# Feed-forward down product of 20 of 32 tiles by seven block products for eight, with the rows of the sum streamed through SBUF

## The chip, the core and the metric

The kernel runs on one core of one Trainium2 chip. The metric is the device time of one execution in microseconds (us). TensorE multiplies into PSUM (eight banks per partition), VectorE and ScalarE take the results out of PSUM, GpSimd does a little elementwise work, and the SP queue issues the DMAs. Each engine works through its own queue in order and waits on semaphores.

## What is computed

One decoder layer for a prompt of 1024 tokens and 8 single-token samples, so 1032 columns in all, with a model width of 1024 and a feed-forward width of 4096. The part that is changed is the feed-forward block near the end:

```python
x = layer_norm(ALPHA * x + (1 + g1) * m, ln1_g, ln1_b)
v = x * (1 + sc2) + sh2
hid = jnp.square(jax.nn.relu(jnp.einsum('bld,df->blf', v, w_up)))
x = layer_norm(ALPHA * x + (1 + g2) * jnp.einsum('blf,fd->bld', hid, w_down), ln2_g, ln2_b)
```

Here `hid` is 4096 wide (32 tiles of 128 features), and the down product adds its 1024 outputs (8 rows of 128 features, `x1[0]` to `x1[7]`, each 128x1032) to the residual.

## The kernel before

All matrices are held transposed: 128 features on the partitions, 1032 columns along the row. Every fp32 operand is split into a high and a low part (`split`: ScalarE writes the high part, VectorE subtracts), and a product of a 128x128 weight tile with a tile of data is three matmuls: high by high, low by high, high by low (`term`, L210 in the profile).

`product` runs over three column blocks of 344 (`BLOCKS`). For each block it takes one PSUM tile from `psm()`, accumulates all its terms there, and calls an evacuation: ScalarE's relu for an up product (24 matmuls a block), VectorE's `gate_add` (L789, and L792 for the 8 sample columns) for a down product. `psm()` draws from a pool of four PSUM tiles of one bank each (tag `mm`); three more (`pss()`, tag `sm`) serve small products.

Weights come by DMA in a list, `order`, two ahead of their use; `parts` splits each into `whi` and `wlo` (two buffers each). The feed-forward runs in 5 groups of four up products and four `wda` weights (each for two output rows, 4 feature tiles), then 2 groups of six up products and eight `wdb` weights. All eight rows `x1` stay in SBUF. A scheduler sets the order of the queues, outside a few stretches that are written out by hand (the last one among them).

Names: L210 is the matmul of `term` (L255 after the change), L202 is `split` (L247 after), L944 the evacuation of an up product (L1047 after), L789 `gate_add` (L834 after), L1115 the matmul and L1090 the addition of the new block products.

Of the kernel before, what the change touches and what calls it, by code (L numbers as in the profile page):

```python
# [10 lines left out]
F32 = mybir.dt.float32  # L11
# [40 lines left out]
SLOTS = {"raw": 2, "whi": 2, "wlo": 2, "G": 2, "xg": 2, "yc": 2}  # L52


NFB = 2
NFA = (DFF // P - 6 * NFB) // 4

# [7 lines left out]
def cols(ap, b):  # L65
    return ap[:, b[0]:b[1]]


def build(tc, ctx, a):
# [7 lines left out]

    cp = ctx.enter_context(tc.tile_pool(name="cp", bufs=1))
    sp = ctx.enter_context(tc.tile_pool(name="sp", bufs=1))
    pm = ctx.enter_context(tc.tile_pool(name="pm", bufs=MMB, space=PSUM))  # L80
    pq = ctx.enter_context(tc.tile_pool(name="pq", bufs=7 - MMB, space=PSUM))
    dp = ctx.enter_context(tc.tile_pool(name="dp", bufs=1, space=DRAM))

# [9 lines left out]
    def tmp(w=T, dt=F32):  # L93
        return sp.tile([P, w], dt, tag="t", name=nm("t"), bufs=5)

    def psm():
        return pm.tile([P, 512], F32, tag="mm", name=nm("mm"))

    def psa():
        return pq.tile([P, 512], F32, tag="ada", name=nm("ada"), bufs=1)  # L100
# [40 lines left out]
    def part(tag, dt, w):  # L141
        return sp.tile([P, w], dt, tag=tag, name=nm(tag), bufs=SLOTS.get(tag, 1))
# [24 lines left out]
    for f in range(NFA):  # L167
        order += [("wup", i) + ((("raw", "aw", "yt"),) if i == 2 else ()) for i in range(4 * f, 4 * f + 4)]
        order += [("wda", f, mp) for mp in range(4)]
    spare = [f"U{i}" for i in range(8, 14)] + ["C0", "C1", "C2", "C3", "G", "G"]  # L170
    for f in range(NFB):
        order += [("wup", 4 * NFA + 6 * f + i) for i in range(6)]
        for m in range(8):
            tags = ("raw", spare[2 * m - 4], spare[2 * m - 3])
            order.append(("wdb", f, m) + ((tags,) if f == NFB - 1 and m > 1 else ()))
    ahead = []

    queue = []
# [9 lines left out]
    def prefetch():  # L188
        if order:
            key, raw = load_next()  # L190
            ahead.append((key, parts(*raw)))

    def weights(*key):
        if not ahead:
            prefetch()
        got, w = ahead.pop(0)
        assert got == key, (got, key)
        prefetch()
        return w
# [782 lines left out]
    for k in range(8):  # L982
        after(rescale(k, b), vcopy)

    for f in range(NFA):
        kh = [t[2] for t in two] if f == 0 else []
        kh += [hidden(4 * f + i) for i in range(len(kh), 4)]
# [6 lines left out]
    def row_shift():  # L994

        near, base = tmp(dt=F32R), tmp()
        nc.scalar.copy(near, x1[0])
        for b in BLOCKS:
            ln1.total(base, (cols(near, b),), P, b, w=rones)
        return base  # L1000

    for f in range(NFB):
        if f == NFB - 1:
            base = row_shift()
        kh = []
        for i in range(6):
            kh.append(hidden(4 * NFA + 6 * f + i))
            if f == NFB - 1:
                for m in ((0, 1), (2, 3, 4), (5, 6, 7), (), (), ())[i]:
                    tc.keep_in_program_order(tt(x1[m], x1[m], base, op=ALU.subtract))  # L1010
        kf = [(i, h, l) for i, (h, l) in enumerate(kh)]
        if f < NFB - 1:
            for m in range(8):
                product(weights("wdb", f, m), kf, lambda b, ps: gate_add(x1[m], ps, M_G2, m, b))
            continue
# [12 lines left out]
        def add_q(m, b):  # L1028
            tt(cols(qsum, b), cols(qsum, b), sq[m], op=ALU.add)

        def moments(b, xs=(), qs=()):

            mu, s, q = cols(mean, b), cols(rsum, b), cols(qsum, b)
            total(mean, (s, *(cols(x1[m], b) for m in xs)), D, b)
            act(s, mu, AF.Square)
            total(qsum, (q, *(sq[m] for m in qs)), D, b, eps)

        def variance(b):
            s, q, w = cols(rsum, b), cols(qsum, b), cols(tmp(), b)
# [24 lines left out]

        wd = []

        def down(m, b):
            product(wd[m], kf, lambda b, ps: gate_add(x1[m], ps, M_G2, m, b), (b,))
            square(m, b)

        b = LAST[0]
        for m in range(8):
            wd.append(weights("wdb", f, m))
# [133 lines left out]
```

## Time and profile before

| | |
|---|---|
| three runs | 1573.47, 1574.13 (median), 1575.65 us |
| profiled execution | 1574.45 us, its span 1572.6 us |
| TensorE busy | 1541.8 us, 98% of the span |
| VectorE busy | 868.6 us, 55% |
| ScalarE busy | 526.3 us, 33% |
| moved by DMA | 141.44 MB, mean 90 GB/s |

The span is the profiled stretch from first to last instruction. A matmul's record lasts longer than the pitch at which matmuls follow each other, since they overlap, so the pitch is read from start to start.

### The profile page before, as it was taken

Reading aid. Unit: us, or ns where it says so; the run is one execution under the profiler, and the core shown is the slowest. Engines: PE = TensorE matmul, PEld = TensorE weight load, DVE = VectorE, ACT = ScalarE, POOL = GpSimd, SP = SyncE. Lnnn points to the kernel's source line nnn. Section 1 sums busy time; section 2 is a strip of 40 time slices with the busy share of each in tenths; the row PEclk is TensorE's granted clock in tenths of the full one; section 3 lists DMA queues with packets and bytes.
Section 4 is the critical chain, followed back from the end, with each engine's and each line's share of the span. In section 5 each row is a group of like instructions: output and inputs, shape, how many; then the busy total and the mean of one; then the engine's idle time right before and its main releaser. Section 6 shows DMA issues by size and latency. Waiting matters only on the chain.

```text
span 1572.6 us, 23959 instructions
## 1 busy us (share of the span) xinstructions
PE 1541.8 (98%) x10058; PEld 1489.2 (95%) x10058; DVE 868.6 (55%) x1653; ACT 526.3 (33%) x805; POOL 169.0 (11%) x168
## 2 busy tenths in 40 slices
PE   6999999999999999999999999999999999999996
PEld 5899999999889999999999999999999999999995
DVE  4575556677876742636996444434343433335477
ACT  2553323323333353613577121121312213113334
POOL 0004222221211311100241000000000000000001
PEclk9999999999999999999999999999999999999998
DMA  9332344344343323412221111111111111111102
GB/s 366 114 118 94 108 132 141 118 140 132 135 151 128 119 96 108 175 42 93 82 68 54 41 54 41 48 47 42 53 41 54 41 54 34 45 56 51 61 31 88
DMA packets 49628, 141.44 MB, mean 90 GB/s; under 512 B 5736, under 2 KB 14696, under 8 KB 49520
## 3 DMA queue, kind: packets, MB, share of 16 engines
q1 hardware_dynamic: 49520, 139.91, 27.4%
q8 instruction: 79, 1.29, 0.3%
q14 instruction: 29, 0.24, 0.1%
HBM read 126.33 MB, written 13.56 MB: 89 GB/s over the span
## 4 chain that ended last, share of the span: by engine, by line
PE 94%; DVE 3%; DMA 1%; ACT 1%; issue 1%; POOL 0%; SPq 0%; ACTq 0%; DVEq 0%; POOLq 0%
PE mm L210 86%; PE ada L229 2%; PE sm L651 1%; PE sm L643 1%; PE sm L842 1%; PE sm L638 1%; PE sm L673 1%; PE sm L210 1%; DMA S<-in_xT 0%; PE sm L617 0%; DVE U L1055 0%; PE sm L236 0%; DMA s<-in_ssm 0%; PE sm L597 0%; PE mm L425 0%
## 5 line engine op out<-in xcount | busy, mean ns | idle before, releaser
L210 PE MATMUL mm<-U,whi 128*128 128x344 f32 x3058 | 778.5, 323 | 4.6 <-ACT U L336 4.6
L210 PEld LDWEIGHTS mm<-U,whi 128*128 128x128 f32 x3058 | 536.6, 188 | 21.4 <-issue 11.8
L210 PE MATMUL mm<-U,wlo 128*128 128x344 f32 x1529 | 488.1, 322 | 0.0
L202 ACT CAST whi<-raw 128x1024 fp32r<-128x1024 f32 (+1 forms) x122 | 125.7, 1030 | 544.0 <-PE mm L210 529.8
L210 PEld LDWEIGHTS mm<-U,wlo 128*128 128x128 f32 x1529 | 286.9, 188 | 3.0 <-issue 2.8
L789 DVE SCALAR_TENSOR_TENSOR U<-mm,mod,U 128x344 f32<-128x344 f32 (+3 forms) x216 | 122.7, 571 | 206.5 <-PE mm L210 206.5
L210 PE MATMUL mm<-S,whi 128*128 128x344 f32 (+3 forms) x912 | 232.8, 320 | 0.0
L202 DVE TENSOR_TENSOR wlo<-raw,whi 128x1024 fp32r<-128x1024 f32 (+1 forms) x122 | 146.5, 1201 | 132.2 <-ACT whi L202 131.8
L210 PEld LDWEIGHTS mm<-S,whi 128*128 128x128 f32 x912 | 160.6, 188 | 0.3
L210 PE MATMUL mm<-S,wlo 128*128 128x344 f32 (+3 forms) x456 | 145.3, 320 | 0.0
L210 PE MATMUL mm<-C,whi 128*128 128x344 f32 x516 | 143.0, 320 | 0.0
L944 DVE TENSOR_TENSOR t<-t 128x344 f32<-128x344 f32 x96 | 49.3, 515 | 87.5 <-ACT t L944 87.5
L210 PEld LDWEIGHTS mm<-C,whi 128*128 128x128 f32 x516 | 92.9, 188 | 0.1
L210 PEld LDWEIGHTS mm<-S,wlo 128*128 128x128 f32 x456 | 85.6, 188 | 0.1
L1057 POOL TENSOR_SCALAR U<-U,vec 128x392 f32<-128x392 f32 (+1 forms) x4 | 5.6, 1388 | 720.0 <-DVE U L1055 720.0
L210 PE MATMUL mm<-C,wlo 128*128 128x344 f32 x258 | 82.5, 320 | 0.0
L210 PE MATMUL mm<-G,whi 128*128 128x344 f32 x258 | 82.1, 321 | 0.1
L210 PE MATMUL mm<-xg,whi 128*128 128x344 f32 x258 | 82.0, 320 | 0.0
L387 DVE SCALAR_TENSOR_TENSOR t<-t,vec,t 128x1064 f32<-128x1064 f32 (+1 forms) x52 | 71.8, 1388 | 10.7 <-ACT t L385 9.7
L944 ACT ACTIVATE t<-mm 128x344 f32<-128x344 f32 x96 | 43.6, 455 | 97.0 <-PE mm L210 97.0
L210 PE MATMUL mm<-yc,whi 128*128 128x344 f32 x210 | 66.8, 322 | 0.0
L945 DVE TENSOR_TENSOR S<-t,S 128x344 fp32r<-128x344 f32 x66 | 33.9, 516 | 29.6 <-ACT S L944 29.3
(360 smaller groups left out, 2117.7 us busy)
## 6 DMA issues: line engine op xcount, KB each, us to landing
raw<-in_win SPq DMA_DIRECT2D x44, 512.0 KB, 3.7
aw<-in_wada SPq DMA_DIRECT2D x33, 512.0 KB, 4.2
raw<-in_wup SPq DMA_DIRECT2D x32, 512.0 KB, 3.5
raw<-in_wout SPq DMA_DIRECT2D x24, 512.0 KB, 3.5
raw<-in_wda SPq DMA_DIRECT2D x20, 512.0 KB, 3.5
G<-acd SPq DMA_DIRECT2D x16, 512.0 KB, 3.9
raw<-in_wdb SPq DMA_DIRECT2D x16, 384.0 KB, 3.1
S<-in_xT SPq DMA_DIRECT2D x8, 516.0 KB, 10.2
```

Source lines behind the costliest of these rows:

```text
L202: return nc.scalar.copy(thi, src), tt(tlo, src, thi, op=ALU.subtract)
L210: mm(ps[:, :b[1] - b[0]], wt, cols(xt, b), start=(i == 0 and q == 0), stop=(i == n - 1 and q == 2))
L229: mm(ps[32 * g:32 * g + 32, :256], cs[:, 2 * kp + k2, :], w[:, c:c + 256], start=(kp == 0), stop=(kp == KD // 2 - 1), tile_position=(0, 32 ...
L387: stt(r, t[:, k:k + n], wt(k), r, op0=ALU.mult, op1=ALU.add)
L638: mm(po[:, i * P:(i + 1) * P], st[:, h0:h0 + P], bc[2 + g][:, sl], start=True, stop=True)
L643: mm(py[r * HD:(r + 1) * HD, i * P:(i + 1) * P], xg[g][:, 0, h * HD:(h + 1) * HD], Gs[g][:, h, :], start=True, stop=True, tile_position=(0 ...
L651: mm(pst, bt[:, g * P:(g + 1) * P], xg[g][:, 1], start=True, stop=True)
L673: mm(pn[:, :BW], w, cols(src, b), start=(i == 0), stop=(i == len(srcs) - 1))
L789: stt(dst[:, lo:hi], ps[:, :hi - lo], mod[:, row + m, 0:1], dst[:, lo:hi], op0=ALU.mult, op1=ALU.add)
L842: mm(pn, w, src, start=(i == 0), stop=(i == len(srcs) - 1))
L944: return [lambda: act(x, ps, AF.Relu), lambda: tt(x, x, x, op=ALU.mult), lambda: nc.scalar.copy(xh, x), lambda: tt(xl, x, xh, op=ALU.subtr ...
L945: lambda: tt(xl, x, xh, op=ALU.subtract)]
```

## The change

Twenty of the 32 feature tiles (five groups of four) are taken by the seven-product scheme for 2x2 blocks: for a pair of output rows, four feature tiles and half the columns of the prompt, blocks of weights and of data are added and subtracted first, then seven block products replace eight. A block product is 12 matmuls of 258 columns (`QW`), 84 for a pair of rows where there were 72 of 344. Products are accumulated on top of each other in PSUM, and VectorE adds the running sum to a row after each (`add_rows`). The eight rows are stored to DRAM (`x1d`) and come back two at a time. Operands of a group are prepared by `operands`, the blocks of weights by `seven_parts`. One up product stands after each of the first two pairs of a group, one or two ahead of the group. The other twelve tiles keep the old product, six at the beginning and six at the end. `psm()` now hands out quarters of one PSUM tile of four banks, `large`, instead of four tiles, for every product of the kernel; the pairs `u` and `v` are halves of it.

```diff
-    pm = ctx.enter_context(tc.tile_pool(name="pm", bufs=MMB, space=PSUM))
+    pm = ctx.enter_context(tc.tile_pool(name="pm", bufs=1, space=PSUM))
...
+    large = pm.tile([P, MMB, 512], F32, tag="mm", name="mm")
+    turn = [0]
+
     def psm():
-        return pm.tile([P, 512], F32, tag="mm", name=nm("mm"))
+        turn[0] += 1
+        return large[:, (turn[0] - 1) % MMB]
...
-            ahead.append((key, parts(*raw)))
+            ahead.append((key, parts(*raw) if key[0] != "wds" else seven_parts(raw[0])))
...
+    def seven_parts(raw):
...
+        ha, la = part("whi", F32R, 768), part("wlo", F32R, 768)
+        hb, lb = part("U2", F32R, 1024), part("U3", F32R, 1024)
+        a11, a12, a22, a21 = (raw[:, 256 * i:256 * i + 256] for i in range(4))
+        (s1, s2), (s3, s4) = ([t[:, :256], t[:, 256:]] for t in (part("wb", F32, 512), part("wc", F32, 512)))
+        tt(s3, a11, a21, op=ALU.subtract)
...
+        pieces(raw[:, :256], ha, la, "a11")
+        pieces(s3, hb[:, :256], lb[:, :256], "s3")
...
-        for mp in range(4):
-            w = weights("wda", f, mp)
-            for m in (2 * mp, 2 * mp + 1):
-                product(w, [(4 * (m % 2) + i, h, l) for i, (h, l) in enumerate(kh)],
-                        lambda b, ps: gate_add(x1[m], ps, M_G2, m, b))
...
+        product(weights("wdb", 0, m), kf, lambda b, ps: gate_add(x1[m], ps, M_G2, m, b))
+        nc.gpsimd.tensor_copy(eight[:, m], x1[m][:, TP:])
+        dma(x1d[m], x1[m])
...
+    def hidden_raw(i):
+        r = tmp()
+        product(weights("wup", i), kv, lambda b, ps: act(cols(r, b), ps, AF.Relu))
+        tt(r, r, r, op=ALU.mult)
+        return r
...
+            split(a_[:, 0], *(x[:, c:c + QW] for x in sops["b11"]))
+            t = tmp()
+            t1, t3, t2, t4 = (t[:, i * QW:(i + 1) * QW] for i in range(4))
+            tt(t1, a_[:, 1], a_[:, 0], op=ALU.subtract)
+            tt(t3, b_[:, 1], a_[:, 1], op=ALU.subtract)
+            tt(t2, b_[:, 1], t1, op=ALU.subtract)
+            tt(t4, b_[:, 0], t2, op=ALU.subtract)
+            w = slice(2 * QW * p, 2 * QW * p + 2 * QW)
+            split(rb[:, w], *(x[:, w] for x in hl["b2"]))
+            split(t[:, :2 * QW], *(x[:, w] for x in hl["odd"]))
+            split(t[:, 2 * QW:], *(x[:, w] for x in hl["even"]))
...
+    def add_rows(ps, row, m, h):
...
+        d, g = four(row)[:, :, h], mod[:, M_G2 + m, 0:1]
+        if isinstance(ps, list):
+            for p in range(2):
+                stt(d[:, p], ps[p][:, :QW], g, d[:, p], op0=ALU.mult, op1=ALU.add)
+            return
+        if h:
+            tt(acc8[:, m], acc8[:, m], ps[:, 1, QW - NS:QW], op=ALU.add)
+        stt(d, ps[:, :, :QW], g, d, op0=ALU.mult, op1=ALU.add)
+
+    def load_rows(mp):
+        rows = [slab(f"U{4 + m % 4}") for m in (2 * mp, 2 * mp + 1)]
+        for i, r in enumerate(rows):
+            dma(r, x1d[2 * mp + i])
+        return rows
...
+            rows[0] = load_rows((mp + 1) % 4)
...
+        def multiply(ps, a_, b_, first=False):
+            for p in range(2):
+                for j in range(2):
+                    wh, wl = (t[:, j * P:(j + 1) * P] for t in w[a_])
...
+                    for q, (wt, xt) in enumerate(((wh, xh), (wl, xh), (wh, xl))):
+                        mm(pp[:, :QW], wt, xt, start=first and j == 0 and q == 0, stop=(j == 1 and q == 2),
+                           skip_group_check=not first)
...
+        u, v = (large[:, 2 * i:2 * i + 2] for i in ((1, 0) if mp % 2 else (0, 1)))
+        y = [pss(), pss()]
+        multiply(u, "a11", "b11", True)
+        add_rows(u, r1, m1, 0)
+        multiply(v, "s3", "t3", True)
+        add_rows(v, r2, m2, 1)
+        multiply(u, "s2", "t2")
+        add_rows(u, r2, m2, 0)
+        multiply(y, "a12", "b21", True)
+        add_rows(y, r1, m1, 0)
+        multiply(u, "s1", "t1")
+        add_rows(u, r2, m2, 1)
+        multiply(v, "a22", "t4")
+        add_rows(v, r2, m2, 0)
+        multiply(u, "s4", "b22")
+        add_rows(u, r1, m1, 1)
...
+            for m, r in ((m1, r1), (m2, r2)):
+                dma(x1d[m], r)
...
+        operands(0, r[0], r[1])
...
+        more = [hidden_raw(nxt[0])]
+        operands(1, r[2], r[3])
         for mp in range(4):
...
+            seven(f, mp)
+            if mp < 2:
+                turn[0] = 2 - 2 * mp
+                more.append(hidden_raw(nxt[1 + mp]))
```

The first place is TensorE's queue in an up product of the feed-forward (its three blocks begin with the data tile `yc`; `mm_...` is the PSUM tile; a bracket names the semaphore that the instruction waits for). Before:

```order
L210 MATMUL mm_10362<-yc_6815,whi_10163 128x344 [waits DVE_49,Activation_49]
...
L210 MATMUL mm_10391<-yc_6815,whi_10163 128x344 [waits Activation_49]
...
L210 MATMUL mm_10420<-yc_6815,whi_10163 128x344 [waits Activation_49]
...
L210 MATMUL mm_10458<-yc_6815,whi_10262 128x344 [waits Activation_49]
L210 MATMUL mm_10458<-yc_6815,wlo_10263 128x344 [waits DVE_49]
...
L210 MATMUL mm_10487<-yc_6815,whi_10262 128x344 [waits Activation_49]
```

The same place of the change:

```order
L255 MATMUL mm<-yc_6659,whi_8976 128x344 [waits Activation_49]
L255 MATMUL mm<-yc_6659,wlo_8977 128x344 [waits DVE_49]
...
L255 MATMUL mm<-U_685_6688,whi_8976 128x344
L255 MATMUL mm<-yc_6659,whi_8976 128x344 [waits Activation_49]
...
L255 MATMUL mm<-U_685_6688,whi_8976 128x344
L1115 MATMUL sm_9417<-S_897_9242,whi_9142 128x258 [waits Activation_49]
L1115 MATMUL sm_9418<-S_897_9242,whi_9142 128x258
L255 MATMUL mm<-yc_6659,whi_9059 128x344 [waits Activation_49]
```

A block begins with a wait for ScalarE in both. The count of the semaphore tells which evacuation is meant: before, `mm_10487` waits for the relu that reads `mm_10362`, four tiles earlier; in the change each block waits for the relu of the block just ahead of it. Two matmuls of a block product into another PSUM tile (`sm`) have moved between two blocks.

The second place is TensorE's queue in the seven block products of one pair of rows, from the second product on (12 matmuls each, the first of each shown, but for the product of `s1`, whose row reads like the first; `mm` is `large`). There is nothing like it before the change.

```order
L1115 MATMUL mm<-S_899_9244,U_891_9144 128x258 [waits DVE_49]
...
L1115 MATMUL mm<-S_901_9246,U_891_9144 128x258 [waits DVE_49]
...
L1115 MATMUL mm<-S_901_9246,whi_9142 128x258 [waits DVE_49]
...
L1115 MATMUL mm<-S_897_9242,U_891_9144 128x258 [waits DVE_49]
...
L1115 MATMUL sm_9627<-S_897_9242,whi_9391 128x258 [waits Activation_49]
L1115 MATMUL sm_9628<-S_897_9242,whi_9391 128x258
```

By their counts, each of the five products into `mm` waits for VectorE's addition (L1090) of the product just ahead, into whichever half of `large` that went. The product into `sm` of the next pair has moved behind the last one.

The third place is ScalarE's queue around the third block of an up product. Before:

```order
L944 ACTIVATE t_11891<-mm_11927 128x344 [waits PE_49]
L944 CAST S_1395_11889<-t_11891 128x344 [waits DVE_49]
L202 CAST whi_11894<-raw_11892 128x1024 [waits DMAHW2_49,PE_49,Activation_49]
L944 ACTIVATE t_11891<-mm_11956 128x344
L944 CAST S_1395_11889<-t_11891 128x344 [waits DVE_49]
```

And in the change, with `whi` the weight that is split two products ahead of its use:

```order
L1047 ACTIVATE t_11992<-mm 128x344 [waits PE_49]
L247 CAST U_1147_12079<-t_12096 128x516 [waits DVE_49]
L247 CAST whi_11995<-raw_11993 128x1024 [waits DMAHW4_49,PE_49]
L1047 ACTIVATE t_11992<-mm 128x344
L247 CAST whi_12109<-raw_12107 128x256 [waits DMAHW0_49,PE_49]
```

In both, the cast of a weight stands ahead of the evacuation of the third block, and the evacuation carries no wait of its own, because the cast waits for the same last matmul.

## Rows read from the trace of the kernel before

**Rows 1.** The page, busy time by engine: us, share of span, instructions.
```profile
PE 1541.8 (98%) x10058; PEld 1489.2 (95%) x10058; DVE 868.6 (55%) x1653; ACT 526.3 (33%) x805; POOL 169.0 (11%) x168
```
**Rows 2.** The page, the chain that ended last, shares by engine.
```profile
PE 94%; DVE 3%; DMA 1%; ACT 1%; issue 1%; POOL 0%; SPq 0%; ACTq 0%; DVEq 0%; POOLq 0%
```
**Rows 3.** Busy time by stretch: PE, PEld, DVE, ACT, POOL (instructions); clock, DMA share, GB/s.
```profile
700.00:800.00 100.00, 99.44 (x621) 97.89 (x621) 76.73 (x147) 47.64 (x76) 18.63 (x14) 1.00 0.26 80
900.00:1000.00 100.00, 100.00 (x637) 100.00 (x636) 41.28 (x80) 20.30 (x33) 0.00 (x0) 1.00 0.15 48
```
**Rows 4.** Waits of PE: waited for, us in total, times, longest.
```profile
PE ada L229 <- DMA C<-in_wada: 5.5, 3, 4.9
PE mm L210 <- ACT U L336: 4.6, 1, 4.6
```
**Rows 5.** Timeline of PE, 256-column blocks: start us, length us, what, count.
```profile
1542.58 1.58 PE L210 MATMUL mm<-S,U 128*128 128x256 f32 x12
1544.00 0.51 PE L210 MATMUL mm<-U,U 128*128 128x256 f32 x3
1544.35 0.40 PE L210 MATMUL mm<-yt,U 128*128 128x256 f32 x2
1544.59 0.28 PE L210 MATMUL mm<-st,U 128*128 128x256 f32 x1
1544.71 1.58 PE L210 MATMUL mm<-S,U 128*128 128x256 f32 x12
```
**Rows 6.** Timeline at the end of a down block, PE and DVE.
```profile
1002.04 0.32 PE L210 MATMUL mm<-S,whi 128*128 128x344 f32 x1
...
1002.20 0.32 PE L210 MATMUL mm<-U,whi 128*128 128x344 f32 x1
...
1002.40 0.58 DVE L789 SCALAR_TENSOR_TENSOR U<-mm,mod,U 128x344 f32<-128x344 f32 x1 [1.05 <-PE mm L210]
```
**Rows 7.** Timeline where PE does wait for an evacuation by ACT.
```profile
29.75 1.05 PE L229 MATMUL ada<-xg,cs 128*32 128x256 f32 x16
...
30.92 0.37 ACT L234 COPY asb<-ada 128x256 f32<-128x256 f32 x1 [4.21 <-PE ada L229]
...
31.34 0.66 PE L236 MATMUL sm<-ident,asb 128*128 128x128 f32 x4 [0.55 <-ACT asb L234]
```
**Rows 8.** Timeline where PE waits for DVE.
```profile
1556.88 0.42 DVE L1026 TENSOR_TENSOR xg<-xg,U 128x256 f32<-128x256 f32 x1
...
1557.45 0.67 PE L842 MATMUL sm<-xg,ones 128*128 128x256 f32 x2 [3.36 <-DVE xg L1026]
```
**Rows 9.** Timeline of ACT at the third block of an up product.
```profile
1040.31 1.05 ACT L202 CAST whi<-raw 128x1024 fp32r<-128x1024 f32 x1 [2.30 <-PE mm L210]
...
1041.26 0.45 ACT L944 ACTIVATE t<-mm 128x344 f32<-128x344 f32 x1
```
**Rows 10.** Groups of ACT by shape: count, busy us, mean ns, idle before.
```profile
L944 ACT ACTIVATE t<-mm 128x344 f32<-128x344 f32 x96 | 43.6, 455 | 97.0 <-PE mm L210 97.0
...
L202 ACT CAST whi<-raw 128x768 fp32r<-128x768 f32 x10 | 8.4, 836 | 50.2 <-PE mm L210 50.2
```
**Rows 11.** Groups of DVE by shape.
```profile
L789 DVE SCALAR_TENSOR_TENSOR U<-mm,mod,U 128x344 f32<-128x344 f32 x128 | 73.3, 574 | 121.6 <-PE mm L210 121.6
...
L789 DVE SCALAR_TENSOR_TENSOR U<-mm,mod,U 128x256 f32<-128x256 f32 x8 | 3.8, 479 | 0.0
...
L792 DVE TENSOR_TENSOR gs<-mm,mod 128x8 f32<-128x8 f32 x72 | 11.2, 156 | 0.0
```
**Rows 12.** DMA issues: queue, count, KB each, us to landing.
```profile
ycd<-yc SPq DMA_DIRECT2D x8, 516.0 KB, 3.1
...
t<-ycd SPq DMA_DIRECT2D x8, 516.0 KB, 4.6
```
**Rows 13.** Busy time by stretch at the start, as in rows 3.
```profile
10.00:15.00 5.00, 0.64 (x4) 0.40 (x4) 3.46 (x9) 2.86 (x3) 0.00 (x0) 0.68 1.02 408
20.00:25.00 5.00, 4.45 (x51) 3.50 (x44) 1.92 (x9) 0.68 (x2) 0.00 (x0) 1.00 1.02 409
```

More of the change, by code (lines that the diff above doesn't have):

```diff
@@ L52 @@
 SLOTS = {"raw": 2, "whi": 2, "wlo": 2, "G": 2, "xg": 2, "yc": 2}
-NFB = 2
-NFA = (DFF // P - 6 * NFB) // 4
+NFS = 5
+NF = 6
+SPAIR = 0, 2, 1, 3
+QW = T // 4
 BLOCKS = [(b * BW, (b + 1) * BW) for b in range(NB)]
@@ L166, in build, with up @@
             order.append(("wout", 1, m) + ((("raw", f"S{m}", f"S{m + 1}"),) if m % 2 == 0 else ()))
-    for f in range(NFA):
-        order += [("wup", i) + ((("raw", "aw", "yt"),) if i == 2 else ()) for i in range(4 * f, 4 * f + 4)]
-        order += [("wda", f, mp) for mp in range(4)]
-    spare = [f"U{i}" for i in range(8, 14)] + ["C0", "C1", "C2", "C3", "G", "G"]
[L171 to L175, printed above, removed]
+    def up(i):
+        return [("wup", i) + ((("raw", "aw", "yt"),) if i == 2 else ())]
+    for i in range(NF):
+        order += up(i)
+    order += [("wdb", 0, m) for m in range(8)]
+    for f in range(NFS):
+        n = NF + 4 * f
+        order += (up(n) if f == 0 else []) + [x for i in SPAIR[f > 0 and 3 or 1:] for x in up(n + i)]
+        nxt = [n + 4 + i for i in (SPAIR if f < NFS - 1 else range(4))]
+        order += up(nxt[0])
+        for mp in range(4):
+            order.append(("wds", f, mp))
+            if mp < 2:
+                order += up(nxt[1 + mp])
+    for i in range(3, NF):
+        order += up(NF + 4 * NFS + i)
+    spare = [f"U{i}" for i in range(8, 14)] + ["C0", "C1", "C2", "C3", "G", "G"]
+    for m in range(8):
+        tags = ("raw", spare[2 * m - 4], spare[2 * m - 3])
+        order.append(("wdb", 1, m) + ((tags,) if m > 1 else ()))
     ahead = []
@@ L190, in prefetch, with pieces @@
             key, raw = load_next()
-            ahead.append((key, parts(*raw)))
+            ahead.append((key, parts(*raw) if key[0] != "wds" else seven_parts(raw[0])))
[5 more added lines that the diff above has]
+        tt(s3, a11, a21, op=ALU.subtract)
+        tt(s1, a21, a22, op=ALU.add)
+        tt(s2, s1, a11, op=ALU.subtract)
+        tt(s4, a12, s2, op=ALU.subtract)
+        got = {}
+        def pieces(src, h, l, *names):
+            w = 256 * len(names)
+            split(src, h[:, :w], l[:, :w])
+            for i, k in enumerate(names):
+                got[k] = h[:, 256 * i:256 * i + 256], l[:, 256 * i:256 * i + 256]
+        pieces(raw[:, :256], ha, la, "a11")
+        pieces(s3, hb[:, :256], lb[:, :256], "s3")
+        pieces(s2, hb[:, 256:512], lb[:, 256:512], "s2")
+        pieces(raw[:, 256:768], ha[:, 256:], la[:, 256:], "a12", "a22")
+        pieces(s1, hb[:, 512:768], lb[:, 512:768], "s1")
+        pieces(s4, hb[:, 768:], lb[:, 768:], "s4")
+        return got
     def weights(*key):
@@ L1002, in build @@
[L1002 to L1015, printed above, removed]
+    eight = cp.tile([P, 8, NS], F32, tag="ysm", name="eight")
@@ new lines, in build, with four @@
+    x1d = [dp.tile([P, T], F32, tag=f"x1d{m}", name=f"x1d{m}") for m in range(8)]
+    kh = [t[2] for t in two] + [hidden(i) for i in range(2, NF)]
+    kf = [(i, h, l) for i, (h, l) in enumerate(kh)]
+    for m in range(8):
+        product(weights("wdb", 0, m), kf, lambda b, ps: gate_add(x1[m], ps, M_G2, m, b))
+        nc.gpsimd.tensor_copy(eight[:, m], x1[m][:, TP:])
+        dma(x1d[m], x1[m])
+    def four(t):
+        return t.rearrange("p (a h c) -> p a h c", a=2, h=2)
+    def hidden_raw(i):
[3 more added lines that the diff above has]
+        return r
@@ new lines, in build, with operands @@
+    sops = {}
+    def operands(j, ra, rb):
+        if j == 0:
+            sops["b11"] = pair(("S0", "S1"))
+        tags = {"b2": (("S2", "S3"), ("U14", "U15")), "odd": (("S4", "S5"), ("yt", "st")), "even": (("S6", "S7"), ("U0", "U1"))}
+        hl = {k: pair(t[j]) for k, t in tags.items()}
+        for k, names in (("b2", ("b21", "b22")), ("odd", ("t1", "t3")), ("even", ("t2", "t4"))):
+            for h, name in enumerate(names):
+                sops[name, j] = [four(t)[:, :, h] for t in hl[k]]
+        for p in range(2):
+            a_, b_ = four(ra)[:, p], four(rb)[:, p]
+            c = (2 * j + p) * QW
+            split(a_[:, 0], *(x[:, c:c + QW] for x in sops["b11"]))
[9 more added lines that the diff above has]
+            split(t[:, 2 * QW:], *(x[:, w] for x in hl["even"]))
@@ new lines, in build @@
+    acc8 = cp.tile([P, 8, NS], F32, tag="xsm", name="acc8")
+    nc.vector.memset(acc8, 0.0)
+    def add_rows(ps, row, m, h):
[7 more added lines that the diff above has]
+        stt(d, ps[:, :, :QW], g, d, op0=ALU.mult, op1=ALU.add)
@@ new lines, in load_rows, with seven @@
+    def load_rows(mp):
[3 more added lines that the diff above has]
+        return rows
+    def seven(f, mp):
+        w = weights("wds", f, mp)
+        m1, m2 = 2 * mp, 2 * mp + 1
+        (r1, r2), last = rows[0], f == NFS - 1
+        if mp < 3 or not last:
+            rows[0] = load_rows((mp + 1) % 4)
+        def multiply(ps, a_, b_, first=False):
+            for p in range(2):
+                for j in range(2):
+                    wh, wl = (t[:, j * P:(j + 1) * P] for t in w[a_])
+                    if b_ == "b11":
+                        xh, xl = (t[:, (2 * j + p) * QW:(2 * j + p + 1) * QW] for t in sops["b11"])
+                    else:
+                        xh, xl = (t[:, p] for t in sops[b_, j])
+                    pp = ps[p] if isinstance(ps, list) else ps[:, p]
+                    for q, (wt, xt) in enumerate(((wh, xh), (wl, xh), (wh, xl))):
[17 more added lines that the diff above has]
+        add_rows(u, r1, m1, 1)
+        if last and mp > 1:
+            x1[m1], x1[m2] = r1, r2
+        else:
+            for m, r in ((m1, r1), (m2, r2)):
+                dma(x1d[m], r)
@@ new lines, in build @@
+    rows = [load_rows(0)]
+    r = [hidden_raw(NF + i) for i in SPAIR]
+    for f in range(NFS):
+        n = NF + 4 * f
+        nxt = [n + 4 + i for i in (SPAIR if f < NFS - 1 else range(4))]
+        if f:
+            turn[0] = 0
+            r.append(hidden_raw(n + SPAIR[3]))
+        operands(0, r[0], r[1])
+        turn[0] = 1
+        more = [hidden_raw(nxt[0])]
+        operands(1, r[2], r[3])
+        for mp in range(4):
+            seven(f, mp)
+            if mp < 2:
+                turn[0] = 2 - 2 * mp
+                more.append(hidden_raw(nxt[1 + mp]))
+        r = more
@@ new lines, in build @@
+    turn[0] = 0
+    kh = []
+    for x in r:
+        h, l = pair(ht[hn % len(ht)])
+        hn += 1
+        split(x, h, l)
+        kh.append((h, l))
+    for m in range(4):
+        x1[m] = slab(f"U{m}")
+        dma(x1[m], x1d[m])
+    tt(acc8, acc8, mod[:, M_G2:M_G2 + 8, 1:9], op=ALU.mult)
+    tt(acc8, acc8, eight, op=ALU.add)
+    for m in range(8):
+        nc.gpsimd.tensor_copy(x1[m][:, TP:], acc8[:, m])
+    for i in range(3, NF):
+        kh.append(hidden(NF + 4 * NFS + i))
+        if i == 3:
+            near, base = tmp(dt=F32R), tmp()
+            nc.scalar.copy(near, x1[0])
+            for b in BLOCKS:
+                ln1.total(base, (cols(near, b),), P, b, w=rones)
+        for m in ((0, 1), (2, 3, 4), (5, 6, 7))[i - 3]:
+            tc.keep_in_program_order(tt(x1[m], x1[m], base, op=ALU.subtract))
@@ L1016, in build @@
+    kf = [(i, h, l) for i, (h, l) in enumerate(kh)]
+    if ks:
         total = ln1.total
@@ L1072, in build @@
         for m in range(8):
-            wd.append(weights("wdb", f, m))
+            wd.append(weights("wdb", 1, m))
             down(m, b)
@@ L1165 @@
     a["wup"] = c_(g["w_up"][0].reshape(KD, P, 32, P).transpose(2, 1, 0, 3)).reshape(32, P, 1024)
-    wd, cut = g["w_down"][0], 4 * NFA * P
-    a["wda"] = c_(wd[:cut].reshape(NFA, 4, P, 4, 2, P).transpose(0, 3, 2, 4, 1, 5)).reshape(NFA, 4, P, 1024)
-    a["wdb"] = c_(wd[cut:].reshape(NFB, 6, P, 8, P).transpose(0, 3, 2, 1, 4)).reshape(NFB, 8, P, 768)
+    wd = g["w_down"][0].reshape(32, P, 8, P)
+    ends = np.stack([wd[:NF], wd[32 - NF:]])
+    a["wdb"] = c_(ends.transpose(0, 3, 2, 1, 4)).reshape(2, 8, P, NF * P)
+    mid = wd[NF:32 - NF].reshape(NFS, 2, 2, P, 4, 2, P)
+    mid = np.stack([mid[:, h, :, :, :, m] for h, m in ((0, 0), (1, 0), (1, 1), (0, 1))])
+    a["wds"] = c_(mid.transpose(1, 4, 3, 0, 2, 5)).reshape(NFS, 4, P, 1024)
     a["vec"] = c_(np.concatenate(
```

9 lines of the change are left out of this document (removed).

## The prediction

> **What bounds the kernel now.** I read the page first: TensorE is busy for 98% of the span [rows 1], and the chain that ended last lies on TensorE for 94% [rows 2]. Two stretches of the view by stretch show the same from inside: all 100 us busy in the plain feed-forward (900 to 1000), with 637 matmuls at the full clock, and 99.44 us in the second half of the mixer's output product and first norm (700 to 800), where VectorE is busy for 76.73 [rows 3]. The waits of TensorE, longest first, begin with a DMA and a cast at the start of the program, 5.5 and 4.6 us; no evacuation stands among the large ones [rows 4]. So the reader is to see an engine that never waits for its results to be taken away. Time saved on TensorE is time saved, and any wait put into its queue is paid in full.
>
> **What the change saves.** A 344-column matmul follows the last one after 100 / 637 = 0.157 us [rows 3]. The 256-column ones at the end of the program follow at (1544.71 - 1542.58) / 18 = 0.1183 us [rows 5]. That is 0.44 ns a column, so 258 columns take 0.1192. A pair of rows took 72 x 0.157 = 11.30 us and takes 84 x 0.1192 = 10.01. Twenty pairs (five groups of four) save 25.8 us.
>
> **What it adds on TensorE's queue.** In the built order every block waits for the evacuation of the block just ahead, where it used to wait for the one four tiles back: the four banks are now one tile, and the program orders a matmul into one quarter behind the read of another. This touches every product of the kernel, not only the twenty pairs. Following the counts of the semaphores, 318 waits of TensorE stand with no other matmul between the block that is read and the block that waits; before, the nearest such wait had 13 or more matmuls between. Of the 318, 116 wait for ScalarE (relu and copies of up and input products), 102 for VectorE's additions and multiplications of a 344-column block (32 of them with the 8 sample columns behind), 100 for the additions L1090 of the block products. A further 73 have one to six matmuls between.
>
> The price of one such pause, step by step. The last matmul's record runs 0.32 us and the next would start 0.16 after it began, so 0.16 us is lost until it ends [rows 6]. The reader starts 0.04 us later where VectorE is free (1002.36 to 1002.40) [rows 6], 0.12 where ScalarE copies `ada` (30.80 to 30.92) [rows 7]; I take 0.08. TensorE starts 0.05 us after ScalarE's end (31.29 to 31.34) [rows 7] and 0.15 after VectorE's (1557.30 to 1557.45) [rows 8]; I take 0.05 and 0.10. In between lies the evacuation itself.
> - ScalarE: relu 0.455 [rows 10], pause 0.16 + 0.08 + 0.455 + 0.05 = 0.75, x116 = 87 us.
> - VectorE, 344 columns: 0.574 [rows 11], pause 0.91, x70 = 64 us. With the sample columns 0.156 more [rows 11], half of it overlapped: 0.99, x32 = 32 us.
> - L1090 takes 2 x 258 columns at once; the trace has no such row. From 0.479 at 256 and 0.574 at 344 columns [rows 11], 1.08 ns a column gives 0.76. Half of these have the sample sum (0.156) ahead of them. Pause 0.16 + 0.08 + 0.76 + 0.08 + 0.10 = 1.18, x100 = 118 us.
> - Weight casts. ScalarE's queue has the cast of a weight ahead of the third block's evacuation. The trace shows what that does: cast at 1040.31, relu only at 1041.26, hidden then by the four tiles [rows 9]. 37 of the 116 stand behind such a cast, 1.05 us each: 39 us. Ten of the 73 stand behind two casts of a `wds` weight, 768 columns together, 0.836 [rows 10], and pause for 0.75 + 0.84: 16 us.
> - The other 63 of the 73 are covered in part: 0.35 us each, 22 us.
> - VectorE's and ScalarE's queues hold other work, so some evacuations come late: 20 us, chosen between nothing and 73 (202 waits for VectorE, 60% busy between the shares of rows 3, half of a 1.2 us instruction left).
>
> Bounds. At the low end the shortest hops (0.04 and 0.05) and nothing for the last three items but the casts of 39: 81 + 84 + 101 + 39 = 305. At the high end the longest hops (0.12 and 0.15), casts 55, partial cover 0.5 us, the full 73: 103 + 105 + 127 + 55 + 36 + 73 = 499. I take 87 + 64 + 32 + 118 + 39 + 16 + 22 + 20 = 398, nearer the middle, since nothing in the rows picks an end.
>
> **What costs nothing, and its cover.** A pair needs on VectorE six L1090 (4.6 us), two additions out of `sm` (1.0), three sample sums (0.5) and nine 256-column and one 512-column instruction for the weights (at most 0.48 and 0.76): 11 us; `operands` costs some 18 a group and four squarings with four weight splits 9. A group is 4 x 11 + 27 = 71 us against 4 x 10.0 + 4 x 11.3 = 85 on TensorE even without pauses, so VectorE is not the bound, only late at single places. If that cover failed, `operands` would show before the first pair of each group, at most 18 us x 5. The rows: a store lands in 3.1 us and a load in 4.6 [rows 12], 7.7 in turn, and a slot has one whole pair, 10 us or more, for both; uncovered they would cost up to 7.7 x 20 = 154 us. The stores on SP's queue wait for VectorE's last addition and stand ahead of the next weights; those are due a pair later.
>
> **Sum.** The profiled execution took 1574.45 us, 0.3 more than the median of the three runs. 1574.45 - 25.8 + 398 = 1946 us. Its own range is 1574.45 - 25.8 + 305 = 1854 to 2048, say 1845 to 2055.
>
> **The rivals.**
>
> *The waits do not bind: faster.* It would need each wait to be satisfied when TensorE comes to it, as if its count meant the evacuation four quarters back. In the trace TensorE does start the next block (1002.20) before VectorE reads the last one (1002.40) without harm [rows 6]. Then the 25.8 us stand, less some microseconds at the start of a group: 1574 - 26 + 4 = 1552. It decides from 26 / 318 = 0.08 us a pause downwards, which the evacuation's own 0.455 us rules out once the count is as the order has it. Chance 5%.
> The Trainium skill, PSUM — Partial Sum Buffer, section "PSUM bank collisions raise a hardware error", says that engines must be kept apart on the same bank and quadrant of partitions, and that different banks run clean. By that rule no pause would be needed here and the time would be 1552; but the semaphore is in the program whether the chip needs it or not.
>
> *The pauses also cost the clock: slower still.* The granted clock was 0.68 over a stretch (10 to 15 us) in which TensorE worked 0.64 of 5 us, and 1.00 in one (20 to 25) with 4.45 of 5 and gaps of half a microsecond [rows 13]. In a block product it would work 1.43 of 2.6 us, between the two. At 1.2 GHz for 2.4 the 1680 matmuls of the block products cost 258 / 2.4 = 107.5 ns more each, 181 us: 1946 + 181 = 2127. For it speaks the low share of work, against it that no pause is longer than 2 us. Chance 9%.
> The Trainium skill, TensorE: Matmul & The Clock Gate, section "A second HAM failure mode: psum-queue depth-cycling", tells of a kernel whose clock swings between its two levels because TensorE idles briefly between groups of matmuls. That would be this rival's 2127; the stretch from 20 to 25 us has such gaps and keeps the full clock.
>
> *The pauses are covered by half more than I count*, because the scheduler slips other matmuls (into `sm`) between blocks in the mixer's part, or the hops overlap: about 150 us less, 1796. Chance 6%.
>
> **How the numbers follow.** Forecast 80%, time 1946. The range 1845 to 2055 holds nearly all of it and a little of its neighbours, about 8 in 10. Faster by over 0.2% (3 us, about what the runs tell from no change) is the first rival, 0.05; within 0.2% needs the pauses to come to just the saving, 0.01; slower 0.94.
>
> **What the profile after would show.** TensorE's busy share falls to about four fifths, and its list of waits is led by relu (L1047) and the additions (L834, L1090), some 0.5 to 0.8 us of idle time a time, a hundred times each. The 258-column matmuls follow at 0.119 us inside a product. The stretch of the mixer, which the seven products do not touch, is longer too, by about an eighth (98 of the 318 pauses with their casts, some 100 us in 840). The clock stays at 1.00. The prediction is wrong if TensorE starts a block while the evacuation ahead still runs, if the mixer takes as long as before, or if TensorE waits for rows or `operands` instead.

## The result, and the profile after

The changed kernel takes 2066.31 us (median of four runs, 2056.94 to 2072.61) against 1574.02 for the kernel before: a ratio of 1.312, interval 1.3075 to 1.3165. The direction and the mechanism were as forecast. The size was not: 492 us more instead of 372, which lies 11 us above the range. The profiled execution took 2068.58 us, its span 2066.6.

The page, busy time by engine, answers to [rows 1]:

```profile
PE 1669.0 (81%) x10298; PEld 1514.2 (73%) x10298; DVE 993.1 (48%) x1904; ACT 570.8 (28%) x921; POOL 157.4 (8%) x184
```

The waits of TensorE (waited for, us in total, times, longest) answer to [rows 4]. What stood there is still there, far down; above it stand evacuations.

```profile
PE mm L1115 <- DVE U L1090: 91.8, 101, 2.7
PE mm L255 <- DVE U L834: 48.6, 56, 5.6
PE mm L255 <- DVE gs L837: 33.1, 32, 3.5
PE mm L255 <- ACT t L989: 27.7, 23, 9.1
PE mm L255 <- ACT t L1047: 27.1, 44, 1.5
PE mm L255 <- ACT t L781: 21.9, 20, 4.7
PE mm L1115 <- ACT t L1047: 15.1, 10, 1.5
...
PE sm L718 <- DVE t L247: 12.6, 8, 5.2
...
PE sm L518 <- DVE t L510: 10.1, 1, 10.1
```

One pause, in the timeline of a pair (start, length, engine, what; in brackets the idle time before). It answers to [rows 6]:

```profile
1303.00 0.28 PE L1115 MATMUL mm<-st,U 128*128 128x258 f32 x1
1303.32 0.16 DVE L1089 TENSOR_TENSOR acc<-acc,mm 128x8 f32<-128x8 f32 x1 [0.89 <-PE mm L1115]
1303.40 0.76 DVE L1090 SCALAR_TENSOR_TENSOR U<-mm,mod,U 128x516 f32<-128x516 f32 x1
1304.21 0.63 PE L1115 MATMUL mm<-S,U 128*128 128x258 f32 x3 [0.93 <-DVE U L1090]
1304.67 0.52 PE L1115 MATMUL mm<-U,U 128*128 128x258 f32 x3
1305.03 0.52 PE L1115 MATMUL mm<-S,U 128*128 128x258 f32 x3
```

The addition takes 0.76 us, as estimated, and TensorE idles for 0.93 us. Then look at the starts: the three matmuls of 1304.67 are followed after 0.36 us, 0.12 each; the three right after the pause, at 1304.21, after 0.46. So the first matmul after a pause costs 0.10 us more than its pitch. Over the 321 pauses at the full clock where this can be read the median is the same 0.10 (113 at 258 columns, 208 at 344).

By stage (columns as in [rows 3]; the border is the first relu of the feed-forward), before and then after:

```profile
0.00:836.00 836.00, 819.84 (x5506) 770.14 (x5507) 533.19 (x998) 330.73 (x461) 161.67 (x162) 1.00 0.39 126
836.00:1572.00 736.00, 721.97 (x4554) 719.07 (x4552) 335.42 (x656) 195.58 (x345) 7.36 (x6) 0.99 0.15 49
```
```profile
0.00:1054.00 1054.00, 885.01 (x5525) 794.96 (x5525) 533.68 (x999) 340.83 (x463) 145.30 (x162) 0.96 0.31 100
1054.00:2066.00 1012.00, 783.95 (x4775) 719.19 (x4773) 459.43 (x905) 229.93 (x458) 12.11 (x22) 0.95 0.25 81
```

The feed-forward is 276 us longer, where the forecast had some 272. The mixer, which has no block product in it, is 218 longer, where the forecast had some 100. So all of the miss lies in the mixer as a sum, though not as single terms (below). And the clock is not 1.00: 0.96 and 0.95.

Why a pause in the mixer can be long, in its timeline:

```profile
806.25 4.90 DVE L828 SCALAR_TENSOR_TENSOR S<-S,vec,t 128x1032 f32<-128x1032 f32 x4
...
807.17 0.32 PE L255 MATMUL mm<-U,whi 128*128 128x344 f32 x1
...
811.35 1.23 DVE L140 SCALAR_TENSOR_TENSOR t<-t,yc 128x1032 f32<-128x1032 f32 x1
812.49 0.57 DVE L834 SCALAR_TENSOR_TENSOR U<-mm,mod,U 128x344 f32<-128x344 f32 x1
...
813.12 0.66 PE L255 MATMUL mm<-C,whi 128*128 128x344 f32 x1 [5.63 <-DVE U L834]
```

The block is done at 807.5; its addition stands in VectorE's queue behind four instructions of a norm (4.90 us together) and three more, and TensorE waits for 5.63 us. Before the change it had three more tiles to go on with, and no wait for an addition stands in its list.

The clock, in the last pair of the first group of block products (by stretch, as above):

```profile
1370.00:1380.00 10.00, 6.70 (x48) 5.97 (x48) 6.88 (x15) 3.70 (x9) 0.00 (x0) 1.00 0.55 189
1380.00:1385.00 5.00, 1.78 (x13) 1.50 (x12) 3.44 (x10) 0.00 (x0) 0.00 (x0) 0.92 0.45 150
1385.00:1397.00 12.00, 8.79 (x36) 7.95 (x36) 4.18 (x8) 2.88 (x6) 0.00 (x0) 0.50 0.24 76
1397.00:1410.00 13.00, 11.60 (x59) 11.03 (x60) 7.78 (x18) 3.63 (x8) 0.00 (x0) 0.84 0.39 135
```

```profile
1382.68 0.48 PE L1115 MATMUL mm<-S,U 128*128 128x258 f32 x2 [2.61 <-DVE U L1090]
```

With pauses of 0.9 us it stays at 1.00. After a pause of 2.61 us that ended at 1382.68 (the addition stands in VectorE's queue behind splits of `operands`, two additions out of `sm` and a subtraction of weight blocks) it is at 0.50, the lower level (1.2 GHz). By the shares of the last three rows (0.8, 12 and 4.2 us) that lasts for 17 us, from 1384.2 to 1401.3, through four more pauses of 0.9 to 1.3 us and into the next up product. The same happens near 1515, 1650 and 1780, the last pairs of the next three groups, and for shorter times (3.4 to 10 us) at fourteen places in the mixer. Of the 19 waits of over 2 us behind the first 30 us, 17 stand at such a stretch. Length alone does not decide: a wait of 3.49 us that ended at 1013.80 left the clock where it was.

```profile
1013.80 0.40 PE L255 MATMUL mm<-yc,whi 128*128 128x344 f32 x1 [3.49 <-DVE U L834]
```
```profile
1010.00:1015.00 5.00, 1.51 (x10) 1.26 (x10) 5.00 (x11) 3.43 (x7) 1.31 (x1) 1.00 0.17 67
```

### The profile page after: what moved, and what is told of

Read it like the earlier page. It is cut to its first block, busy times and chain, and to the rows that moved or that the text cites. A ratio compares the mean times of both kernels' runs of the same rounds, so it can differ in the third digit from the quotient of the medians.

```text
span 2066.6 us, 25030 instructions
## 1 busy us (share of the span) xinstructions
PE 1669.0 (81%) x10298; PEld 1514.2 (73%) x10298; DVE 993.1 (48%) x1904; ACT 570.8 (28%) x921; POOL 157.4 (8%) x184
## 3 DMA queue, kind: packets, MB, share of 16 engines
q8 instruction: 80, 1.31, 0.3%
## 5 line engine op out<-in xcount | busy, mean ns | idle before, releaser
L247 ACT CAST whi<-raw 128x1024 fp32r<-128x1024 f32 (+2 forms) x142 | 123.0, 879 | 798.5 <-PE mm L255 443.7
L247 DVE TENSOR_TENSOR wlo<-raw,whi 128x1024 fp32r<-128x1024 f32 (+2 forms) x142 | 143.8, 1019 | 318.4 <-ACT whi L247 316.8
L1115 PE MATMUL mm<-S,U 128*128 128x258 f32 x480 | 96.9, 313 | 72.5 <-DVE U L1090 68.8
L834 DVE SCALAR_TENSOR_TENSOR U<-mm,mod,U 128x344 f32<-128x344 f32 (+3 forms) x96 | 55.0, 572 | 194.5 <-PE mm L255 194.3
L1115 PEld LDWEIGHTS mm<-S,U 128*128 128x128 f32 x480 | 72.8, 202 | 89.1 <-DVE U L1090 59.3
L1090 DVE SCALAR_TENSOR_TENSOR U<-mm,mod,U 128x516 f32<-128x516 f32 x120 | 90.3, 752 | 79.0 <-PE mm L1115 79.0
L255 PEld LDWEIGHTS mm<-yc,whi 128*128 128x128 f32 x210 | 40.9, 195 | 94.7 <-ACT t L1047 39.6
L1115 PE MATMUL mm<-S,whi 128*128 128x258 f32 x240 | 60.0, 311 | 38.1 <-DVE U L1090 23.0
L255 PE MATMUL mm<-S,whi 128*128 128x344 f32 (+3 forms) x240 | 65.9, 340 | 24.1 <-DVE U L834 11.4
L1115 PEld LDWEIGHTS mm<-S,whi 128*128 128x128 f32 x240 | 43.3, 198 | 47.4 <-DVE U L1090 28.5
L255 PEld LDWEIGHTS mm<-S,whi 128*128 128x128 f32 x240 | 43.4, 192 | 32.8 <-DVE U L834 16.9
```

What stands on the lines that cost most here:

```text
L247: return nc.scalar.copy(thi, src), tt(tlo, src, thi, op=ALU.subtract)
L255: mm(ps[:, :b[1] - b[0]], wt, cols(xt, b), start=(i == 0 and q == 0), stop=(i == n - 1 and q == 2))
L834: stt(dst[:, lo:hi], ps[:, :hi - lo], mod[:, row + m, 0:1], dst[:, lo:hi], op0=ALU.mult, op1=ALU.add)
L1090: stt(d, ps[:, :, :QW], g, d, op0=ALU.mult, op1=ALU.add)
L1115: mm(pp[:, :QW], wt, xt, start=first and j == 0 and q == 0, stop=(j == 1 and q == 2), skip_group_check=not first)
```

## The experiments

All are compared with the kernel before, run on the same chip (1574.9 us for the first four, 1574.3 for the others). Where a run is set against the changed kernel, that is its 2066.3 us; its four runs lie 16 us apart, so a difference of a few microseconds between two of these times says nothing.

**The shared tile alone**, in the kernel before, without block products:

```diff
-    pm = ctx.enter_context(tc.tile_pool(name="pm", bufs=MMB, space=PSUM))
+    pm = ctx.enter_context(tc.tile_pool(name="pm", bufs=1, space=PSUM))
...
-        return pm.tile([P, 512], F32, tag="mm", name=nm("mm"))
+        turn[0] += 1
+        return large[:, (turn[0] - 1) % MMB]
```

> The kernel before with one edit: its four PSUM tiles become quarters of one tile; no block products. Theory A (the shared tile makes nearly all of the loss, in every product): the mixer ends near 1054 us as in the changed kernel (836 before), and the 96 up blocks and 168 down blocks of the feed-forward pause for 0.75 and 0.91 us each, with 26 casts of 1.05 us ahead: 72 + 157 + 27 = 256. Time 1574 + 218 + 256 = 2048, between 1990 and 2100. Rival B (the block products, their operands and the streamed rows make a good part of the loss themselves): the feed-forward is hardly longer than before, time 1800 to 1900.

Measured 2061.17 us, ratio 1.3085 (1.3066 to 1.3105): theory A, at its upper part. This edit alone makes a loss as large as the whole one, 486 us of 492, without any block product (and without what block products save). The mixer ends at 1050. Its waits:

```profile
PE mm L214 <- DVE U L793: 102.1, 136, 5.7
PE mm L214 <- ACT t L948: 88.7, 93, 9.1
PE mm L214 <- DVE gs L796: 64.1, 72, 2.9
```

**Four tiles, with the block products**, the counterpart:

```diff
-    large = pm.tile([P, MMB, 512], F32, tag="mm", name="mm")
+    large = [pm.tile([P, 512], F32, tag=f"mm{i}", name=f"mm{i}") for i in range(MMB)]
...
-        return large[:, (turn[0] - 1) % MMB]
+        return large[(turn[0] - 1) % MMB]
...
+            if h:
+                tt(acc8[:, m], acc8[:, m], ps[1][:, QW - NS:QW], op=ALU.add)
...
-        u, v = (large[:, 2 * i:2 * i + 2] for i in ((1, 0) if mp % 2 else (0, 1)))
+        u, v = (large[2 * i:2 * i + 2] for i in ((1, 0) if mp % 2 else (0, 1)))
```

> The changed kernel with four PSUM tiles of one bank again; the addition of a block product is then two instructions of 258 columns for one of 516. Theory A: no pause is left, the mixer ends near 836 us, the clock stays at 1.00, and the 25.8 us of the seven products show: 1552, between 1545 and 1565. Rival B (operands, additions or streamed rows bind once the shared tile is gone): waits for S, U or rows at the first pair of each group, 1590 or more.

Measured 1559.88 us, ratio 0.9905 (0.9888 to 0.9921): theory A. This version beats both kernels, the one before by 15 us. Its page and its waits, longest first:

```profile
PE 1525.7 (98%) x10298; PEld 1467.5 (94%) x10298; DVE 1000.0 (64%) x2024; ACT 558.9 (36%) x919; POOL 174.7 (11%) x184
```
```profile
PE ada L274 <- DMA C<-in_wada: 5.5, 3, 4.7
PE mm L1117 <- DVE U L1088: 4.7, 10, 0.8
PE mm L255 <- ACT U L381: 3.7, 1, 3.7
```

The matmuls are as many as in the changed kernel; rows and `operands` are not in the list. The seven products save 15 of the 25.8 us that the pitch promised. The ten waits for the additions take 4.7 of the rest; where the other 6 go stays open. In its timeline TensorE starts the next block product (1063.98) before VectorE takes out the second half of the last one (1064.56), and works on while VectorE reads:

```profile
1063.86 0.28 PE L1117 MATMUL mm<-S,whi 128*128 128x258 f32 x1
...
1063.98 0.52 PE L1117 MATMUL mm<-S,U 128*128 128x258 f32 x3
1064.34 0.40 PE L1117 MATMUL mm<-yt,U 128*128 128x258 f32 x2
1064.56 0.48 DVE L1088 SCALAR_TENSOR_TENSOR U<-mm,mod,U 128x258 f32<-128x258 f32 x1
```

**Two tiles of two banks**, so that the addition stays one instruction:

```diff
-    large = pm.tile([P, MMB, 512], F32, tag="mm", name="mm")
+    large = [pm.tile([P, 2, 512], F32, tag=f"mm{i}", name=f"mm{i}") for i in range(2)]
...
-        return large[:, (turn[0] - 1) % MMB]
+        return large[(turn[0] - 1) // 2 % 2][:, (turn[0] - 1) % 2]
```

> The changed kernel with two PSUM tiles of two banks, each the u or v of a pair, so that the addition stays one instruction of 516 columns. By the order of the program 12 waits stand with no matmul between the block read and the block that waits, and 27 with one to six. Theory A: 12 x 0.9 + 27 x 0.35 = 20 us over the version without false waits, 1572, between 1555 and 1595. Rival B (waits inside a block's tile pair still bind in most products): 1700 or more.

Measured 1655.64 us, ratio 1.0515 (1.0497 to 1.0534): outside both. Its timeline shows TensorE idle 88 times for 82.6 us, against 22 times for 23.1 with four tiles. The count by matmuls in between was the wrong measure: it said nothing of how late an evacuation is in its own queue. 38 of the 88 are shorter than half a microsecond, most of them waits for an evacuation; they make only 12 us. Eleven of over 1.5 us make 38 us (with four tiles there are four, 13.5 us).

**Idle matmuls into the pauses**, 258 columns into the bank of `ada`, unused by then, to see what the clock costs:

```diff
+            for i in range(0 if isinstance(ps, list) else FILL):
+                tc.keep_in_program_order(mm(pad[:, :QW], wh, xh, start=True, stop=True))
```

> The changed kernel with six idle matmuls of 258 columns (0.72 us) into an unused PSUM bank behind each block product that ends in the shared tile: 120 x 6 = 720 more matmuls, 86 us of work. Theory C (the clock falls to its lower level in the first pair of a group because TensorE is idle there for up to 2.6 us, and this makes a good part of what the forecast missed): the granted clock stays at 1.00 in the four stretches near 1385, 1515, 1650 and 1780 us and the time falls by 15 to 35 us although work is added. Rival D (the clock has nothing to do with the pauses, or the added work comes in the way): the clock falls as before, time the same or up to 86 us longer.

Measured 2066.57 us, ratio 1.3122 (1.31 to 1.3144): neither. (The place is the last pair of a group, as above, not the first.) The clock did nearly as theory C says, the time did not. The first of the four places, and the second:

```profile
1375.00:1388.00 13.00, 9.71 (x72) 8.90 (x72) 8.91 (x22) 3.71 (x9) 0.00 (x0) 1.00 0.50 162
1388.00:1397.00 9.00, 8.20 (x62) 7.67 (x63) 2.75 (x7) 1.05 (x1) 0.00 (x0) 1.00 0.23 74
1510.00:1532.00 22.00, 17.98 (x121) 16.75 (x119) 13.33 (x30) 5.41 (x13) 0.00 (x0) 0.92 0.47 151
```

At the first and third place the clock stays at 1.00, at the second and fourth it falls for 3.4 us instead of 17. Matched matmul by matmul, this run is 5.4 us faster from 1385 to 1402 and 4.1 to 5.8 at the three other places, 20 in all; it loses 0.7 us each time the six stand in front of a product into `sm` that was ready.

So the next run has them **only behind five products of the last pair of a group**:

```diff
+            for i in range(FILL if mp == 3 and a_ in ("a11", "s3", "s2", "s1", "a22") else 0):
+                tc.keep_in_program_order(mm(pad[:, :QW], wh, xh, start=True, stop=True))
```

> The changed kernel with the six idle matmuls only behind five products of the last pair of each group, the pair in which TensorE was idle for 2.5 to 2.7 us and the clock fell: 150 matmuls, 18 us of work. The run with 720 gained 5.4 us at each of the four places where the clock had fallen and gave about as much back where the six stood in front of work that was ready. Theory C (the fall of the clock there costs some 5 us each time, and comes from the idle time): the clock stays at 1.00 near 1385, 1515, 1650 and 1780 us and the time falls by 15 to 25 us, to 2041 to 2051. Rival D (the gain of the first run came from something else): 2060 to 2085.

(The "5.4 us at each of the four places" of that text is the first one's value.) Measured 2051.72 us, ratio 1.3021 (1.3002 to 1.3041): 14.6 us less than the changed kernel with 18 us of work added; all four runs lie below all four of it. Matched matmul by matmul, the gain lies at the four places alone (4.7, 5.3, 4.5 and 2.8 us). So rival D is out, and a fall of the clock costs what theory C says, at its low end:

```profile
1380.00:1385.00 5.00, 3.21 (x24) 3.03 (x23) 3.36 (x10) 0.00 (x0) 0.00 (x0) 0.92 0.45 153
1385.00:1397.00 12.00, 10.32 (x68) 9.73 (x67) 6.34 (x13) 3.43 (x7) 0.00 (x0) 0.89 0.31 90
```

The clock falls here too, at three of the four places, but for 3.4 us instead of 17. That the idle time decides it is not shown: the run with the split written later, below, has no matmul added, and there the falls last 3.4 us as well.

**Evacuations ahead of weight casts**, for every ordinary product:

```diff
-            evac(b, ps[:, :b[1] - b[0]])
+            with tc.high_priority():
+                evac(b, ps[:, :b[1] - b[0]])
```

> The changed kernel with the evacuations of the ordinary products put ahead of other work in the order of their queues: the cast of a weight stands ahead of one or two evacuations where there were some 50 of TensorE's waits behind one. It sizes two terms of the forecast, 39 us for 37 casts of 1.05 and 16 us for ten double casts. Theory A (they cost their length): 55 us less, 2011, between 1995 and 2025. Rival E (the cast is then late for the next weight, or TensorE waits elsewhere for the same time): 2045 to 2080.

Measured 2009.12 us, ratio 1.2751 (1.2712 to 1.279): 57 less, the number of theory A, but not from the casts alone. The waits for ScalarE's evacuations fall from 116.6 us to 82.2, so by 34 and not 55; ten waits of products into `sm` for their weight's cast (10.4 us) go too, and the clock's deficit falls from 83 us to 64, worth 12 by the ratio below. The agreement to 2 us is luck. The longest wait for the relu falls from 1.5 us to 0.6:

```profile
PE mm L255 <- ACT t L1048: 26.8, 49, 0.6
```

**The split of the next weight written behind the up product**, only in the feed-forward:

```diff
-        prefetch()
+        if key[0] == "wup" and key[1] > 1:
+            late.append(1)
+        else:
+            prefetch()
...
             evac(b, ps[:, :b[1] - b[0]])
+        if late:
+            late.clear()
+            prefetch()
```

> The changed kernel with the split of the next weight written behind an up product instead of ahead of it, for the feed-forward's up products alone: 30 of the waits for ScalarE lose the cast ahead of them (20 of 1.05 us or 0.84 at full length, 10 with one or two matmuls between). Theory A: 20 to 28 us less, 2038 to 2046. Rival E (the weight is late instead): 2055 to 2080.

Measured 2009.89 us, ratio 1.2767 (1.2742 to 1.2792): 56 less, twice what theory A gives and outside both ranges. The scheduler ordered the mixer anew as well: it is 26 us shorter (first relu at 1028.6). The feed-forward is 34 shorter, and part of that is the clock: at the four places it comes back after 3.4 us instead of 17, and over the kernel its deficit falls from 83 us to 41. So this run doesn't size the casts.

**Four tiles, additions first:**

```diff
-            if h:
-                tt(acc8[:, m], acc8[:, m], ps[1][:, QW - NS:QW], op=ALU.add)
-            for p in range(2):
-                stt(d[:, p], ps[p][:, :QW], g, d[:, p], op0=ALU.mult, op1=ALU.add)
+            with tc.high_priority():
+                for p in range(2):
+                    stt(d[:, p], ps[p][:, :QW], g, d[:, p], op0=ALU.mult, op1=ALU.add)
+                if h:
+                    tt(acc8[:, m], acc8[:, m], ps[1][:, QW - NS:QW], op=ALU.add)
```

> The version with four PSUM tiles, its additions of block products put ahead of other work in VectorE's queue and the sample sum behind them. In the version before it ten waits of TensorE for these additions make 4.7 us. Theory A (they are late in VectorE's queue): the ten waits shrink to 2 us or less, 1557, between 1553 and 1560. Rival F (TensorE has run ahead of VectorE there and the wait only moves): 1560 to 1566.

Measured 1559.68 us, ratio 0.9904 (0.9887 to 0.992): no change. The waits for the additions go from 4.7 us in ten to 3.5 in five, but five waits for the sample sum, now behind them, take 1.1. So the wait has moved, as rival F says, though the time lies in theory A's range; it is too small to tell from the time.

## Why the prediction was right in kind and 120 us short

**The mechanism stands.** Every block waits for the evacuation just ahead, in every product: the shared tile alone gives 2061, four tiles 1560. The timeline after has 390 idle stretches of TensorE (12 before), and 345 of them are waits for an evacuation, where the forecast counted 318 + 73 = 391.

**The rivals.** That the waits do not bind (1552) is near what four tiles show (1560), not one. By the Trainium skill, PSUM — Partial Sum Buffer, section "PSUM bank collisions raise a hardware error", engines on different banks run clean; the run with four tiles (1063.98 beside 1064.56) agrees. It is the order of the built program, which goes by tiles, that asks for the wait. "Covered by half" (1796) is out.

**The terms**, in us over the kernel before:

| term | forecast | in the trace |
|---|---|---|
| seven products for eight | -25.8 | -24 (pitch 0.120) |
| idle time in evacuation waits | 335 (398 less 391 x 0.16) | 321 in 345 waits |
| ends of the last matmuls, 0.16 each | 63 | 60 (378 new pauses) |
| first matmul after a pause, 0.10 each | 0 | 38 |
| other waits of TensorE | 0 | 45 (64 less the 19 of before) |
| clock | 0 | some 47, an estimate |
| sum | 372 | 487 of 494 |

(494 is the difference of the spans.) Term by term the evacuations were priced well, with their ends: additions of block products 1.08 us a pause in 106 (forecast 1.18), VectorE's others 1.07 in 114 (0.91 and 0.99, with lateness and partial cover beside), ScalarE's 1.12 in 125 (87 us and 55 of casts for 126, so 1.13). This last agreement is one of the mean only: by the run with evacuations first the casts are 34 us and not 55, and single long waits, such as the 9.1 us at L989, stand in the same mean.

**What failed.** Three steps.
- "The clock stays at 1.00." The mean clock is 0.960 instead of 0.994, a deficit of 83 - 9 = 74 us at full clock. At the place shown the deficit was 0.4 + 6.0 + 2.1 = 8.5 us and the filler run got 5.4 back there, 0.63 of it; by that ratio 74 become 47. A direct count bears this out: the intervals between matmuls at the lower level, without a pause in them, come to 49 us over their pitch, 3 in the kernel before. The rival with 2127 was right that the clock would fall and wrong on where: it was charged to every block product, where in the stretch shown pauses of 0.9 us leave the clock at 1.00; it falls at most of the few long ones. The forecast held against it that "no pause is longer than 2 us" and did not ask which evacuation would come late behind other work, its own "late only at single places".
  The Trainium skill, TensorE: Matmul & The Clock Gate, section "A second HAM failure mode: psum-queue depth-cycling", puts the loss on frequent short idling between groups of matmuls. This trace agrees only in part: with short pauses alone the clock stayed at 1.00 (1370 to 1380); behind a long one it stayed low through four more short ones.
- The price of a pause had no restart: three steps (end, hop, evacuation) were read from rows 6 to 8, but not the start of the second matmul after a wait.
- "Some 100 us" for the mixer. It took the 98 waits with no matmul between and left the partly covered ones aside: 117 evacuation waits of 1.01 us stand there, with queues that are late as at 812.49 (the 20 us for lateness were for the whole kernel). And it took the mixer's own chains as covered: waits such as `L518` (10.1 us, once) and `L718` (12.6, eight times) stand in the kernel with the shared tile alone too (10.1 and 12.5 us) and not in the kernel before. That TensorE has no blocks in hand any more to cover them is my reading.

In the feed-forward the same omissions (restart 23, clock some 27, other waits 12) were made up by evacuation waits that came to 239 us with their ends, where the forecast left 298 for them; so its 276 against 272 is no sign of a right working.

**Right as forecast:** the addition's 0.75 us, the pitch of 258 columns, and that VectorE, the rows (landing in 3.5 and 4.3 us) and `operands` are not the bound: with four tiles only 4.7 us of waits for the additions are left. In the changed kernel TensorE does wait for `operands` four times (3.8 us) and for the cast of a block weight ten times (10.4 us); both are among the other waits.

## What to carry to other kernels

In this program a PSUM tile over several banks was one object for the scheduler that set the order, whatever quarter a block used: give every block that must overlap with another's evacuation a tile of its own, and pay the second addition instruction (four tiles 1560 us, one tile 2066). When a pause is added many times, price what follows it too (the first matmul, the clock after the longest ones) and look for the evacuations that stand behind long instructions on their engine; the mean pause was forecast well, the tail was not. And work that had been hidden by depth, such as serial chains far from the edit, comes into the open when the depth goes.

## What was not expected of the hardware

- The first matmul after a wait costs 0.10 us more than its pitch (0.22 for 0.12 at 258 columns, 0.26 for 0.157 at 344), as the median of 321 pauses of the changed kernel and 355 of the kernel with the shared tile alone, all at the full clock.
- The granted clock fell from 1.00 to 0.50, 1.5 us after the end of a pause of 2.61 us, and stayed there for 17 us (1384.2 to 1401.3), while TensorE was busy for 13 of them; pauses of 0.9 us in every 2.6 had not moved it, nor did the one of 3.49 us at 1013.80.
- 150 matmuls with no use made the kernel 14.6 us faster; the gain lay at the four places where the clock was now at its lower level for 3.4 us or not at all.
